# First SwiGLU block of a Hymba-style layer: the third of seven matmul products is issued ahead of the second

## The chip, the core and the metric

The kernel runs on one core of a Trainium2 chip. The time is device microseconds (us) of one launch, the median of several runs; shorter is better. The engines are named as in the profile: PE is TensorE (matmuls; PEld is its weight load, which overlaps), ACT is ScalarE, DVE is VectorE, POOL is GpSimd, and SP is the engine whose queue issues most transfers.

## What is computed

One decoder layer on 512 tokens of width 1024, in float32. Cut to what matters here:

```python
def swiglu(x, w_gate, w_up, w_down):
    return (jax.nn.silu(x @ w_gate) * (x @ w_up)) @ w_down

x = x + 0.5 * swiglu(rms_norm(x, g_ffn1), w_ffn1_gate, w_ffn1_up, w_ffn1_down)   # first SwiGLU block
h = rms_norm(x, g_mix); p = h @ w_in                                            # mixing stage:
x = x + concat(attention(p), conv(p), memory_attention(p, mem)) @ w_out         #   three head groups
x = x + 0.5 * swiglu(rms_norm(x, g_ffn2), w_ffn2_gate, w_ffn2_up, w_ffn2_down)   # second SwiGLU block
```

The hidden width D_FF is 2816, which is 22 blocks of 128.

## The kernel before

**Layout.** Activations are kept transposed: features lie on the 128 partitions and the 512 tokens along the free dimension. `x` has 8 such slices. Every float32 factor is split into a high part in the reduced format fp32r and the remainder (`whi`/`wlo` for weights, `bh`/`bl` for activations, `hh`/`hl` for hidden values), and each product is three matmuls: high times high, high times low, low times high.

**One SwiGLU block.** `ffn` loops over the 22 hidden blocks `f`. The first four (`N_DIRECT`) compute gate and up directly. The other 18 go through `fast`, which gets the gate and up values of one hidden block from seven products instead of eight, each over half the features and half the tokens (a Strassen-like scheme). A product is 4 steps of k with 3 matmuls each (lines 444, 445, 446): 12 matmuls of 128x256. In the text of `fast` the seven are, by the name of their activation block: `B_11`, `B_21`, `B_Q1`, `B_Q2`, `B_22`, `B_T4`, `B_T3`. They are called here by these names, without the B_.

**Which accumulator each one uses.** An accumulator bank is 128 partitions by 512 float32. `b` is half of one bank: product 11 fills it, `ACT.copy` (L455) reads it, Q2 is added to it, `ACT.copy` (L461) reads it again, T3 is added and DVE reads it (L475). `de` is a whole bank: product 21 fills its left half, Q1 its right half; `ACT.activation` (L459) reads the right half and writes its negative to `s45`; then 22 is added to the right half, and DVE reads all of `de` (L464). `c` is half of another bank (profile name `sc`) and takes T4. The profile calls `b` and `de` both `mm`, and `s12` and `s45` both `kept`.

**Which weights each one uses.** `W.next()` hands out one split weight tile: `w0` (raw gate weights) serves 11 and 21, `w1` (a sum of weights) serves Q1 and Q2, `w2` serves 22 and T3, `w3` serves T4. A call of `W.next()` also sees to it that the tile three places further on is loaded and split: a cast on ACT (L167), a subtraction on DVE (L168), sums of weights on DVE (L126 to L129), and a transfer issued on SP (L142). There are four slots of `whi`/`wlo` used in turn and four raw tiles. `w3` has a slot of its own (`vhi`/`vlo`).

**Between the products.** `mid` holds the down projections that are spread over the blocks from f = 8 on, and one at f = 5. Down projections of a block are 12 or 24 matmuls in lines 347 to 349: one after product 22, the others after T3. Some values of f also run hooks: preparations of the memory tokens (f = 12 to 18) and of the rotary table (from f = 19).

**Order.** The kernel is written as one program; a scheduler turns it into one queue per engine and puts in the waits between the engines. An instruction that is ready may be placed ahead of one that stands before it in the text. In the mixing stage the text's own order is the list `ORDER`, which begins:

```python
c c c c pM0 pM1 sumM c c facM pK c scoresM00 scoresM01 c softM01 softM00 weightsM0 c sumK c pV scoresM11
```

There `pM0` is a projection of 24 matmuls (L347 to L349), followed by a square on ACT (L817), `sumM` is 16 small matmuls (L826) that read these squares, and `pK` is the next projection.

Of the kernel before, what the change touches and what calls it, by code (L numbers as in the profile page):

```python
# [34 lines left out]
AF = mybir.ActivationFunctionType  # L35
# [47 lines left out]
B_T3, B_Q1, B_Q2, B_T4, B_21, B_22, B_11 = range(7)  # L83
# [124 lines left out]
def layer(tc, ctx, a):  # L208
    nc = tc.nc
    PE, ACT, DVE, POOL = nc.tensor, nc.scalar, nc.vector, nc.gpsimd  # L210
# [12 lines left out]
    def mm_bank():  # L223
        return psum.tile([P, T], F32, tag="mm", name=nm("mm"), bufs=4)

    def sc_bank():
        return psum.tile([P, T], F32, tag="sc", name=nm("sc"), bufs=2)
# [4 lines left out]
    def work():  # L232
        return tmp.tile([P, T], F32, tag="t", name=nm("t"), bufs=5)
# [160 lines left out]
    def ffn(pool, norm, first, gain, hooks, next_gain, last):  # L394
# [5 lines left out]
        def hidden(f, t):  # L400
            h_hi[f], h_lo[f] = atile("hh"), atile("hl")
            ACT.copy(h_hi[f], t)
            DVE.tensor_tensor(h_lo[f], t, h_hi[f].bitcast(F32), op=ALU.subtract)

        def kept():
            return pool.tile([P, T], F32, tag="kept", name=nm("kept"), bufs=3)
# [32 lines left out]
        def product(ps, w, woff, block, first):  # L439
            wh, wl = w  # L440
            for k in range(4):
                c = slice(woff + k * P, woff + (k + 1) * P)
                one, end = first and k == 0, k == 3
                PE.matmul(ps, wh[:, c], bh[k][:, block], start=one, stop=False, skip_group_check=not first)  # L444
                PE.matmul(ps, wh[:, c], bl[k][:, block], start=False, stop=False, skip_group_check=not first)  # L445
                PE.matmul(ps, wl[:, c], bh[k][:, block], start=False, stop=end, skip_group_check=not first)  # L446

        def fast(f, mid):

            l, r = slice(0, 256), slice(256, 512)  # L450
            b, de, c = mm_bank()[:, l], mm_bank(), sc_bank()[:, l]
            s12, s45, g, u = kept(), kept(), work(), work()
            w0 = W.next()
            product(b, w0, 0, B_11, True)
            ACT.copy(s12[:, l], b)  # L455
            product(de[:, l], w0, 512, B_21, True)
            w1 = W.next()
            product(de[:, r], w1, 0, B_Q1, True)
            ACT.activation(s45[:, r], de[:, r], AF.Copy, scale=-1.0)  # L459
            product(b, w1, 512, B_Q2, False)  # L460
            ACT.copy(s12[:, r], b)  # L461
            w2 = W.next()
            product(de[:, r], w2, 0, B_22, False)
            DVE.tensor_tensor(g, de, s12, op=ALU.add)  # L464
            ACT.activation(g, g, AF.Silu)
            rest = []
            for d in mid:
                rest += down(*d)
            if rest:
                rest.pop(0)()  # L470
            w3 = W.next()
            product(c, w3, 0, B_T4, True)
            ACT.copy(s45[:, l], c)
            product(b, w2, 512, B_T3, False)
            DVE.tensor_tensor(  # L475
                u.rearrange("p (a b) -> p a b", a=2), s45.rearrange("p (a b) -> p a b", a=2),
                b.unsqueeze(1).to_broadcast([P, 2, 256]), op=ALU.subtract,
            )
            DVE.tensor_tensor(u, u, g, op=ALU.mult)
            hidden(f, u)  # L480
            for d in rest:
                d()

        def down(r, g):

            lo, hi = ROUNDS[r]
            end = r == len(ROUNDS) - 1
            wh, wl = W.next()

            def step(j):  # L490
                d = g * per_load(r) + j
                cut = last and end and d == KT - 1
                for t0, t1 in [(0, T // 2), (T // 2, T)] if cut else [(0, T)]:
                    ps = mm_bank()[:, : t1 - t0]
                    mm3(
                        ps, wh, wl, range(lo, hi), lambda k: h_hi[k][:, t0:t1], lambda k: h_lo[k][:, t0:t1],
                        True, True, woff=lo - j * (hi - lo), cut=1 + (r > 0 and not cut),
                    )
                    xd = x[:, d, t0:t1]
                    if r == 0 and g < 2:  # L500
                        o = work()
                        ACT.activation(o, ps, AF.Copy, scale=0.5)
                        POOL.dma_start(xd, o, accum_op=ALU.add)
                        continue
                    o = work()[:, : t1 - t0] if last and end else xd
                    DVE.scalar_tensor_tensor(o, ps, 0.5, xd, op0=ALU.mult, op1=ALU.add)  # L506
                    if last and end:
                        nc.sync.dma_start(a["out"][d, :, t0:t1], o)
                if end and not last:
                    nxt.add(d)  # L510
                    scaled_split(d, next_gain)

            return [lambda j=j: step(j) for j in range(per_load(r))]
# [4 lines left out]
        for f in range(NF):  # L518
# [4 lines left out]
            if f >= N_DIRECT:  # L523
                fast(f, mid)
            else:
                g, u = (sc_bank(), sc_bank()) if f % 3 == 2 else (mm_bank(), mm_bank())
                gh, gl = W.next()
                if f == 0:
                    uh, ul = W.next()
                    for ks in first:  # L530
                        mm3(g, gh, gl, ks, xhk, xlk, ks[0] == 0, ks[-1] == 7)
                        mm3(u, uh, ul, ks, xhk, xlk, ks[0] == 0, ks[-1] == 7)
                    norm.stats()
                    held = (g, u)
                else:
                    mm3(g, gh, gl, range(8), xhk, xlk, True, True)
                    if f == 1:
                        norm.spread()
                        raw[0] = evac(0, *held)
                        blocks(0)  # L540
                        hidden(0, raw[0])
                    uh, ul = W.next()
                    mm3(u, uh, ul, range(8), xhk, xlk, True, True)
                    raw[f] = evac(f, g, u)
                    if f == 1:
                        hidden(1, raw[1])
                    blocks(f)
                if f == N_DIRECT - 1:
                    for i in range(2, N_DIRECT):
                        hidden(i, raw[i])  # L550
# [5 lines left out]
        r = len(ROUNDS) - 1  # L556
# [676 lines left out]
```

## Time and profile before

| | |
|---|---|
| runs (three) | 866.07, 872.06, 865.25 us; median 866.07 |
| profiled execution, own time | 870.17 us |
| its span (first to last instruction) | 868.1 us |
| mean granted TensorE clock | 1.000 |
| PE busy | 861.3 us (99%) |
| PEld busy | 795.1 us (92%) |
| DVE busy | 698.3 us (80%) |
| ACT busy | 446.0 us (51%) |
| read from HBM | 85.45 MB |
| fast part of the first SwiGLU block | about 70 to 344 us of the span |
| mixing stage | about 369 to 545 us |
| second SwiGLU block | about 545 us to the end |

How to read it: "busy" is the time in which an engine has an instruction in flight. Matmuls are pipelined, so a matmul of 0.28 us starts every 0.11 us or so, and TensorE's pace is read from the distance between starts, not from durations. A row of the timeline gives start (us), duration (us), engine, line, operation, output and inputs, shape and count; in square brackets stands the idle time of that engine ahead of the instruction, and what released it. A wait row gives the engine and line that waited, for whom, the total, the number of times and the longest.

### The profile page before, as it was taken

To read this page: it belongs to the slowest core of one execution; us is meant where nothing else is said; L and a number is where in the kernel's file an instruction comes from. 1 tells how busy PE (TensorE), PEld (TensorE's weight loads), DVE (VectorE), ACT (ScalarE), POOL (GpSimd) and SP (SyncE) were. 2 spreads that over 40 slices of the span, in tenths; PEclk is the share of its full clock that TensorE was granted. 3 is DMA by queue.
4 is the path that set the end of the run, shared out by engine and by line. 5 is a ranking of instruction groups with operands and counts; after the bars stand their busy time and mean duration, and the time that the engine had idled before them with its cause. 6 is when DMAs were issued, how large, how long until landed. Compare 5 with 4: busy or idle time off the path is not lost.

```text
span 868.1 us, 15720 instructions
## 1 busy us (share of the span) xinstructions
PE 861.3 (99%) x6361; PEld 795.1 (92%) x6361; DVE 698.3 (80%) x1163; ACT 446.0 (51%) x740; POOL 27.9 (3%) x30
## 2 busy tenths in 40 slices
PE   9999999999999999999999999999999999999998
PEld 5889999999999999988776878889999999999998
DVE  7998877777868887869989976997987878787772
ACT  7455545455554454632939754454554444545440
POOL 0010000000000000300000021010000000000000
PEclk9999999999999999999999999999999999999999
DMA  7326334334454344232020333336333333333312
GB/s 271 122 83 165 94 97 122 99 110 134 111 145 146 97 113 130 95 97 62 0 62 13 110 89 84 99 90 159 105 106 121 95 121 85 116 98 99 121 49 99
DMA packets 34809, 91.45 MB, mean 105 GB/s; under 512 B 3248, under 2 KB 5808, under 8 KB 34736
## 3 DMA queue, kind: packets, MB, share of 16 engines
q1 hardware_dynamic: 32000, 85.99, 32.1%
q0 software_dynamic: 1584, 2.88, 2.1%
q10 hardware_dynamic: 1152, 1.57, 0.7%
q8 instruction: 50, 0.82, 0.4%
q14 instruction: 23, 0.19, 0.1%
HBM read 85.45 MB, written 2.10 MB: 101 GB/s over the span
## 4 chain that ended last, share of the span: by engine, by line
PE 92%; DVE 3%; ACT 2%; issue 1%; DMA 1%; SPq 0%; ACTq 0%; DVEq 0%
PE mm L347 15%; PE mm L348 14%; PE mm L349 14%; PE mm L444 11%; PE mm L446 11%; PE mm L445 11%; PE sc L444 2%; PE sc L446 2%; PE sc L445 2%; PE sc L347 1%; PE sc L349 1%; PE sc L348 1%; PE tp L948 1%; PE tp L962 1%; ACT p L913 1%
## 5 line engine op out<-in xcount | busy, mean ns | idle before, releaser
L444 PE MATMUL mm<-bh,whi 128*128 128x256 f32 x864 | 239.9, 278 | 0.2 <-ACT kept L459 0.2
L446 PE MATMUL mm<-bh,wlo 128*128 128x256 f32 x864 | 239.6, 277 | 0.0
L445 PE MATMUL mm<-bl,whi 128*128 128x256 f32 x864 | 239.6, 277 | 0.0
L348 PE MATMUL mm<-hl,whi 128*128 128x256 f32 (+1 forms) x640 | 184.7, 289 | 0.0
L349 PE MATMUL mm<-hh,wlo 128*128 128x256 f32 (+1 forms) x640 | 184.6, 289 | 0.0
L347 PE MATMUL mm<-hh,whi 128*128 128x256 f32 (+1 forms) x640 | 184.1, 289 | 0.0
L167 ACT CAST whi<-wraw 128x1024 fp32r<-128x1024 f32 (+2 forms) x122 | 124.1, 1021 | 106.2 <-PE mm L348 45.0
L168 DVE TENSOR_TENSOR wlo<-wraw,whi 128x1024 fp32r<-128x1024 f32 (+2 forms) x122 | 145.4, 1193 | 34.4 <-ACT whi L167 34.0
L446 PEld LDWEIGHTS mm<-bh,wlo 128*128 128x128 f32 x864 | 163.1, 189 | 0.0
L444 PEld LDWEIGHTS mm<-bh,whi 128*128 128x128 f32 x864 | 162.2, 188 | 0.5 <-ACT kept L459 0.4
L445 PEld LDWEIGHTS mm<-bl,whi 128*128 128x128 f32 x864 | 162.2, 188 | 0.2
L349 PEld LDWEIGHTS mm<-hh,wlo 128*128 128x128 f32 x640 | 120.8, 189 | 2.9
L347 PEld LDWEIGHTS mm<-hh,whi 128*128 128x128 f32 x640 | 120.1, 188 | 2.7
L348 PEld LDWEIGHTS mm<-hl,whi 128*128 128x128 f32 x640 | 120.1, 188 | 2.7
L168 DVE TENSOR_TENSOR wlo<-s,whi 128x1024 fp32r<-128x1024 f32 x72 | 87.9, 1222 | 36.0 <-ACT whi L167 35.6
L167 ACT CAST whi<-s 128x1024 fp32r<-128x1024 f32 x72 | 75.5, 1050 | 47.3 <-PE mm L445 43.5
L348 PE MATMUL mm<-xl,whi 128*128 128x512 f32 x192 | 75.9, 395 | 0.6 <-DVE xl L359 0.5
L347 PE MATMUL mm<-xh,whi 128*128 128x512 f32 x192 | 76.3, 402 | 0.0
L349 PE MATMUL mm<-xh,wlo 128*128 128x512 f32 x192 | 75.8, 395 | 0.0
L506 DVE SCALAR_TENSOR_TENSOR x<-mm,x 128x512 f32<-128x512 f32 x80 | 54.0, 682 | 3.7 <-PE mm L349 3.7
L167 ACT CAST vhi<-wraw 128x512 fp32r<-128x512 f32 x36 | 22.4, 622 | 62.7 <-PE sc L445 48.5
L126 DVE TENSOR_TENSOR s<-wraw 128x512 f32<-128x512 f32 x36 | 24.9, 691 | 32.6 <-DMA wraw<-in_wgu 32.6
(243 smaller groups left out, 1368.3 us busy)
## 6 DMA issues: line engine op xcount, KB each, us to landing
wraw<-in_wgu SPq DMA_DIRECT2D x86, 512.0 KB, 3.6
wraw<-in_wd SPq DMA_DIRECT2D x44, 512.0 KB, 3.7
wraw<-in_win SPq DMA_DIRECT2D x12, 512.0 KB, 3.5
x<-t POOLq DMA_DIRECT2D x8, 256.0 KB, 6.1
out<-t SPq DMA_DIRECT2D x7, 256.0 KB, 2.0
x<-in_xT SPq DMA_DIRECT2D x3, 512.0 KB, 6.6
wraw<-in_wout_a SPq DMA_DIRECT2D x6, 256.0 KB, 2.7
wraw<-in_wgu SPq DMA_DIRECT2D x4, 256.0 KB, 4.9
```

Of the source, the lines that this page charges most:

```text
L126: nc.vector.tensor_tensor(s12[:, l], u[:, l], u[:, r], op=ALU.add)
L167: nc.scalar.copy(hi[:, :cols], raw[:, :cols])
L168: nc.vector.tensor_tensor(lo[:, :cols], raw[:, :cols], hi[:, :cols].bitcast(F32), op=ALU.subtract)
L347: PE.matmul(ps[:, t], wh[:, w], hi(k)[:, t], start=one, stop=False, skip_group_check=cut > 1)
L348: PE.matmul(ps[:, t], wh[:, w], lo(k)[:, t], start=False, stop=False, skip_group_check=cut > 1)
L349: PE.matmul(ps[:, t], wl[:, w], hi(k)[:, t], start=False, stop=end, skip_group_check=cut > 1)
L444: PE.matmul(ps, wh[:, c], bh[k][:, block], start=one, stop=False, skip_group_check=not first)
L445: PE.matmul(ps, wh[:, c], bl[k][:, block], start=False, stop=False, skip_group_check=not first)
L446: PE.matmul(ps, wl[:, c], bh[k][:, block], start=False, stop=end, skip_group_check=not first)
L506: DVE.scalar_tensor_tensor(o, ps, 0.5, xd, op0=ALU.mult, op1=ALU.add)
L913: ACT.activation(self.p[n, h][:, c], src[h][:, i, c], AF.Exp, scale=self.fac[:, m : m + 1], bias=self.neg[:, m : m + 1], accum_out=self.de ...
L948: PE.transpose(ps[:, i * P : (i + 1) * P], self.p[n, h][:, c : c + P], ident)
```

## The change

In `fast`, the call `w1 = W.next()` moves ahead of product 21 (in both SwiGLU blocks). In the first SwiGLU block (`last` is False), Q1 and the reading of its result (L459) then stand in the text ahead of product 21. All else keeps its order. Since Q1 now opens the bank `de`, product 21 is issued without the start flag there; its values are the same.

```diff
             product(b, w0, 0, B_11, True)
             ACT.copy(s12[:, l], b)
-            product(de[:, l], w0, 512, B_21, True)
             w1 = W.next()
-            product(de[:, r], w1, 0, B_Q1, True)
-            ACT.activation(s45[:, r], de[:, r], AF.Copy, scale=-1.0)
+            if last:
+                product(de[:, l], w0, 512, B_21, True)
+                product(de[:, r], w1, 0, B_Q1, True)
+                ACT.activation(s45[:, r], de[:, r], AF.Copy, scale=-1.0)
+            else:
+                product(de[:, r], w1, 0, B_Q1, True)
+                ACT.activation(s45[:, r], de[:, r], AF.Copy, scale=-1.0)
+                product(de[:, l], w0, 512, B_21, False)
             product(b, w1, 512, B_Q2, False)
             ACT.copy(s12[:, r], b)
             w2 = W.next()
```

## Prediction on record

> **What bounds the kernel now.** First the page's busy line and its chain of work, to see which engine sets the end.
>
> ```profile
> PE 861.3 (99%) x6361; PEld 795.1 (92%) x6361; DVE 698.3 (80%) x1163; ACT 446.0 (51%) x740; POOL 27.9 (3%) x30
> PE 92%; DVE 3%; ACT 2%; issue 1%; DMA 1%; SPq 0%; ACTq 0%; DVEq 0%
> ```
>
> TensorE is busy 99% of the span and is 92% of the chain. An edit that changes no matmul can therefore only win or lose TensorE's idle time, or change its pace. So the second view is the busy time of each engine in stretches; this row is the fast part of the first block.
>
> ```profile
> 70.00:344.00 274.00, 273.83 (x2336) 272.47 (x2335) 216.81 (x313) 138.91 (x214) 2.76 (x5) 1.00 0.41 119
> ```
>
> The columns after the length are PE, PEld, DVE, ACT, POOL with counts, then the granted clock. TensorE is busy 273.83 of 274.00 us: 0.17 us of visible idle time in all 18 blocks. The waits of TensorE and of its weight loads in 70:345 name the one place:
>
> ```profile
> PE mm L444 <- ACT kept L459: 0.2, 1, 0.2
> PEld mm L444 <- ACT kept L459: 0.4, 1, 0.4
> ```
>
> One wait, once: product 22 of block f = 8 waits for L459, the negated copy that frees the right half of `de`. The timeline there:
>
> ```profile
> 116.57 0.38 ACT L455 COPY kept<-mm 128x256 f32<-128x256 f32 x1
> 117.83 0.63 ACT L402 CAST hh<-t 128x512 fp32r<-128x512 f32 x1 [0.89 <-DVE t L479]
> 118.36 1.05 ACT L167 CAST whi<-wraw 128x1024 fp32r<-128x1024 f32 x1
> 119.31 0.37 ACT L459 ACTIVATE kept<-mm 128x256 f32<-128x256 f32 x1
> ...
> 119.29 0.28 PE L446 MATMUL mm<-bh,wlo 128*128 128x256 f32 x1
> 119.73 0.39 PE L444 MATMUL mm<-bh,whi 128*128 128x256 f32 x1 [0.17 <-ACT kept L459]
> 119.96 0.28 PE L445 MATMUL mm<-bl,whi 128*128 128x256 f32 x1
> ...
> 119.73 0.19 PEld L444 LDWEIGHTS mm<-bh,whi 128*128 128x128 f32 x1 [0.36 <-ACT kept L459]
> ```
>
> ACT was held up by L402, which waited for DVE; then came a cast; L459 ended at 119.68 and the weight load behind it began 0.05 later. At the usual step of 0.113 us (next fence) the row at 119.96 would have stood at 119.29 + 0.23 = 119.52: the wait costs 0.44 us.
>
> The third reading is TensorE's pace, from the counts in four stretches that hold no wait (the first also holds a few longer matmuls and isn't used):
>
> ```profile
> 70.00:119.00 49.00, 49.00 (x407) 47.83 (x406) 41.67 (x56) 27.64 (x44) 0.00 (x0) 1.00 0.39 114
> 120.00:270.00 150.00, 150.00 (x1276) 150.00 (x1276) 111.55 (x149) 74.70 (x119) 2.58 (x3) 1.00 0.40 118
> 283.00:343.00 60.00, 60.00 (x532) 60.00 (x531) 49.37 (x81) 27.85 (x43) 0.18 (x2) 1.00 0.39 114
> 630.00:760.00 130.00, 130.00 (x1150) 130.00 (x1149) 101.42 (x133) 65.48 (x100) 0.00 (x0) 1.00 0.36 107
> ```
>
> 150/1276 is 117.6 ns a matmul, 60/532 is 112.8 and 130/1150 is 113.0, with the clock at 1.00 and TensorE never idle in all three. The long step begins right behind the wait at 119.7. Over 1276 matmuls, 4.6 ns each are 5.8 us, thirteen times the wait itself. What makes a step long isn't shown; that it began with this wait may be chance, but it is the only wait and the only onset. So 6.2 us of the profiled 870.17 hang on one late L459.
>
> **The change part by part.** *Work.* Nothing is added or removed: 18 blocks of 84 matmuls stay, as do L455, L459 and L461. Sum: 0.
>
> *`w1 = W.next()` moves ahead of product 21, in both blocks.* With it move a cast on ACT, a subtraction on DVE, at times the sums of weights and a transfer on SP. What it passes, product 21, is TensorE's alone, so ACT's, DVE's and SP's queues keep this order: 0. In the second SwiGLU block that is all there is: 0, with no cover to lose.
>
> *Q1 runs a product earlier and 21 a product later, first block.* A product is 12 x 0.113 = 1.36 us. Q1 needs `w1` 1.36 us sooner, and the slot of `w0` comes free up to 1.36 us later, for the next tile. The tightest case is where that tile is the next block's own `w1`:
>
> ```profile
> 107.30 1.05 ACT L167 CAST whi<-s 128x1024 fp32r<-128x1024 f32 x1 [0.16 <-PE mm L445]
> ...
> 108.39 1.23 DVE L168 TENSOR_TENSOR wlo<-s,whi 128x1024 fp32r<-128x1024 f32 x1 [0.16 <-ACT whi L167]
> ```
>
> The cast follows the last reading of `w0` in f = 7 and the tile is split at 109.62. Working back from 119.29 at 1.36 us a product, Q1 of f = 8 starts at 116.68. With the change, split 110.98 and wanted 115.32: 4.3 us of slack are left, so 0. If that cover were gone, each microsecond late would be one of TensorE's. The transfer behind that slot shifts by as much, inside DVE's slack (216.81 busy of 274.00, 3.2 us free a block).
>
> *L455 against Q2.* Q2 may be added to `b` once L455 has read it. Two products lie between 11 and Q2 now. If Q2 follows Q1 directly there is one. In f = 8 L455 ends at 116.95 and Q2 would be wanted at 116.68: 0.3 us late. If 21 keeps its place ahead of Q2: 0.
>
> *L459 against 22.* Now one product of cover (Q2, 1.36 us); in the new text two (21 and Q2). L459 is ready 1.36 us sooner, and the cast ahead of it at 118.36 reads into the slot of `w0`, so it is ready only after 21 and drops behind L459. In f = 8 L459 could then end by 118.4 to 118.8, against 22 wanted at 119.40. The 0.44 us go, and with them, if the onset was no chance, the long step.
>
> *L459 against 21, a new wait.* 21 writes the left half of the bank whose right half L459 reads. The trace before has no row in which TensorE writes one half of a bank while ACT reads the other, so the cost is bounded. From below 0: no wait, or enough of Q2 put between. From above, nothing between, from f = 7:
>
> ```profile
> 108.41 0.28 PE L446 MATMUL mm<-bh,wlo 128*128 128x256 f32 x1
> 108.52 0.28 PE L444 MATMUL mm<-bh,whi 128*128 128x256 f32 x1
> ...
> 108.78 0.38 ACT L459 ACTIVATE kept<-mm 128x256 f32<-128x256 f32 x1 [0.43 <-PE mm L446]
> ```
>
> Q1's last matmul starts at 108.41, L459 ends at 109.16, and with 0.05 as at 119.73 the next matmul starts at 109.21 instead of 108.52: 0.69, and 0.11 for the restart (119.73 to 119.96 is 0.23, not 0.113) make 0.80 us a block, 14.4 us for 18. Behind 21 on TensorE stand 22, T4 and T3, and ACT and DVE wait for those. Seven matmuls of Q2 in between (0.8/0.113) hide it. Would they be put there? In the mixing stage the text has all 16 sums of `sumM` ahead of `pK`; the queue ran otherwise:
>
> ```profile
> 399.35 0.95 PE L826 MATMUL tp<-pair,t 128*128 128x2 f32 x8
> 400.16 0.48 PE L347 MATMUL mm<-xh,whi 128*128 128x512 f32 x1
> ...
> 401.40 0.39 PE L349 MATMUL mm<-xh,wlo 128*128 128x512 f32 x1
> 401.63 0.95 PE L826 MATMUL tp<-pair,t 128*128 128x2 f32 x8
> ...
> 400.32 0.59 ACT L817 ACTIVATE t<-mm 128x512 f32<-128x512 f32 x1
> ```
>
> Six matmuls of `pK` were put in while L817 was outstanding, and the second eight sums came 0.7 us after L817's end at 400.91: enough, with some over. I take 0, the nearest row, and keep 14.4.
>
> On this the Trainium skill, PSUM — Partial Sum Buffer, section "PSUM bank collisions raise a hardware error", speaks against the change: TensorE and ScalarE on one bank collide even at different columns, and the guard has to go by bank. By that rule the wait at 21 exists in each of the 18 blocks; no run here shows it yet.
>
> **Sum.** Against the profiled execution's 870.17: -0.44 - 5.8 = 863.9. The three runs are 865.25, 866.07 and 872.06. The third is 6.4 above the mean of the two others, 865.7, about the 6.2 of the late L459, so I estimate that the two ran without the long step and the profiled execution with it. Against a median of that kind there is little left to win. Forecast: between 863.9 and 865.7, **865.0**.
>
> **The rivals.** *A. Late in f = 8 all the same, and a long step behind it* (about 872). If L459 stays behind L402 on ACT, it takes the cast's place at 118.36 and ends at 118.73; 21 could start at 118.78. With Q1 over at 116.68, TensorE has 1.36 us of Q2 from 117.00 on and waits 0.4 us more, or 1.3 us in all with seven matmuls. So 0.9 to 1.4 us are lost instead of 0.44, and in every run: 865.7 + 5.8 + 1.1 = 872.6, or 870.9 from the profiled 870.17; 872. For it: the row at 117.83, L402 held by DVE. Against it: the cast ahead of L459 goes, and nothing says that L402 stays first.
>
> *B. Slower: TensorE waits for L459 at 21 in each block.* Place: the first weight load of 21; price 0.113 us for each matmul short of seven; it decides as soon as fewer are put in. None put in: 865.7 + 14.4 = 880.1, and with a long step through all 2336 matmuls (10.7 us) 890.8. Half the cover: 873. For it: the shared bank, the rule above. Against it: the sums at 401.63, with 0.7 us over.
>
> *C. The change doesn't do what it says:* TensorE's queue comes out in the old order, and nothing moves: 866.07. For it: as the sums show, a queue needn't follow the text. Against it: nothing keeps Q1 back, its weights are ready 4 us ahead.
>
> **How the numbers follow.** Forecast 0.45; A 0.25; B 0.18 (0.10 of it short waits, up to 876; 0.08 beyond); C 0.10; something faster than 863 0.02. The range is 863 to 876: from 0.9 below the sum against the profiled execution, through A, to the smaller half of B; outside lie B's upper part and the tail below, and part of each case's spread. A measurement of this kernel tells about 1% from no change, 8.7 us: 857.4 to 874.7 counts as the same. Forecast, C and nearly all of A lie inside, B from 5 matmuls short on lies above: faster 0.02, same 0.80, slower 0.18.
>
> **What would show it.** Right: in 70:344 no wait on L459 or L455, Q1's start 1.36 us into each block, and 113 ns a matmul throughout. A: one wait near f = 8 and 117.6 ns behind it. B: "PEld mm L444 <- ACT kept L459" 18 times, 0.1 to 0.7 us each. C: Q1 at 2.72 us into each block. Most likely to make me wrong: that the step's length depends on something other than this wait, or that L459 is placed badly on ACT.

## The result and the profile after

The changed kernel takes **874.78 us** (median of nine runs, 872.38 to 876.73) against 865.91 (nine runs, 865.25 to 872.06): the ratio is **1.0081**, 95% interval [1.0054, 1.0108]. The profiled execution took 875.49 us. First the page's busy line and its chain by engine:

```profile
PE 863.4 (99%) x6361; PEld 794.8 (91%) x6361; DVE 696.2 (80%) x1163; ACT 443.7 (51%) x740; POOL 27.9 (3%) x30
PE 92%; DVE 3%; ACT 2%; DMA 2%; issue 1%; SPq 0%; ACTq 0%; DVEq 0%
```

The counts are those of before: no work came or went. TensorE still sets the end, over a span of 873.2 instead of 868.1 us. To see where the 5.1 us lie, take a line that stands at the border of the first block and the mixing stage, the sums of squares of L378, in the view of one source line, of the kernel before and of the changed one:

```profile
L378 PE MATMUL tp<-ones,sqsum x8: 165/250/250, 376.0 to 376.7; 128*128 128x1 f32 x8
```

```profile
L378 PE MATMUL tp<-ones,sqsum x8: 165/250/250, 381.2 to 381.9; 128*128 128x1 f32 x8
```

They start 5.2 us later, so all of the difference had arisen by then, in the first block. The waits between 60 and 350 us name it (line numbers from the edit on are larger: L459 is now L463):

```profile
PEld mm L444 <- ACT kept L463: 4.9, 16, 1.1
PE mm L444 <- ACT kept L463: 0.9, 1, 0.9
PEld mm L444 <- ACT kept L455: 0.5, 1, 0.5
PE mm L444 <- ACT kept L455: 0.3, 1, 0.3
```

Where the weight load had one wait on the negated copy, it has 16. The timeline at f = 7 shows the usual one (start, duration, engine, line; the idle time before it in brackets):

```profile
108.14 0.28 PE L446 MATMUL mm<-bh,wlo 128*128 128x256 f32 x1
108.25 0.28 PE L444 MATMUL mm<-bh,whi 128*128 128x256 f32 x1
...
108.59 0.74 PE L444 MATMUL mm<-bh,whi 128*128 128x256 f32 x2
109.17 0.29 PE L445 MATMUL mm<-bl,whi 128*128 128x256 f32 x1
...
108.95 0.19 PEld L444 LDWEIGHTS mm<-bh,whi 128*128 128x128 f32 x1 [0.28 <-ACT kept L463]
...
108.51 0.39 ACT L463 ACTIVATE kept<-mm 128x256 f32<-128x256 f32 x1 [1.05 <-PE mm L446]
```

Q1's last matmul starts at 108.14, and ACT reads its result from 108.51 to 108.90. Between Q1 and 21 the queue holds **four** matmuls of Q2 (108.25 to 108.59), in this block and in 14 others; in the three blocks at 214, 230 and 245 us it holds five. The row with x2 is the last of them and 21's first, whose weights are loaded at 108.95, 0.05 us after the read. From 108.59 to 109.17 two steps take 0.58 us instead of 0.23: 0.35 lost. Two blocks lose more. The first fence is f = 8, the second f = 9:

```profile
118.48 0.28 PE L444 MATMUL mm<-bh,whi 128*128 128x256 f32 x1
119.68 0.39 PE L444 MATMUL mm<-bh,whi 128*128 128x256 f32 x1 [0.93 <-ACT kept L463]
...
117.03 0.37 ACT L455 COPY kept<-mm 128x256 f32<-128x256 f32 x1
118.73 0.62 ACT L402 CAST hh<-t 128x512 fp32r<-128x512 f32 x1 [1.32 <-DVE t L484]
119.25 0.38 ACT L463 ACTIVATE kept<-mm 128x256 f32<-128x256 f32 x1
```

```profile
134.19 0.28 PE L446 MATMUL mm<-bh,wlo 128*128 128x256 f32 x1
134.81 0.38 PE L444 MATMUL mm<-bh,whi 128*128 128x256 f32 x1 [0.34 <-ACT kept L455]
...
133.86 0.62 ACT L402 CAST hh<-t 128x512 fp32r<-128x512 f32 x1 [1.09 <-DVE t L484]
134.39 0.36 ACT L455 COPY kept<-mm 128x256 f32<-128x256 f32 x1
```

In both, L402 of the block before stands first on ACT and waits for DVE; in f = 8 it holds up L463 and 21, in f = 9 L455 and Q2. The stretches give the pace:

```profile
70.00:119.00 49.00, 48.44 (x390) 46.31 (x388) 39.35 (x54) 26.46 (x43) 0.00 (x0) 1.00 0.37 107
120.00:270.00 150.00, 149.33 (x1269) 147.72 (x1268) 108.44 (x145) 73.20 (x117) 2.58 (x3) 1.00 0.40 118
283.00:343.00 60.00, 59.74 (x519) 58.95 (x518) 49.20 (x80) 27.64 (x42) 0.00 (x0) 1.00 0.37 110
630.00:760.00 130.00, 130.00 (x1149) 130.00 (x1149) 103.06 (x136) 65.35 (x100) 0.00 (x0) 1.00 0.37 110
```

Before, the first three held 407, 1276 and 532 matmuls. To split waits from pace, I took the starts of all 128x256 matmuls between 70 and 346 us: what a gap has over its steps counts as wait (restart included), what is left over 113.3 ns a step as long step. The kernel before lost 1.9 us in waits and 5.9 in steps, the changed one 8.4 and 3.9. About 1.5 us of the waits are in every kernel below (memory preparation and transposes), so the new order costs about 6.4 us of waits, and its profiled execution had 2 us less of the long step than that of before. That difference gives 4.4 of the 5.1 us. The long step ran here from f = 9 (135 us) to 230 us at 117.8 ns a matmul, was 113.3 to 113.9 in the blocks behind that but for some 6 us at 274 us, which every kernel has (see the first experiment), and came back from 349 to 370 us (180 matmuls of 117.8 ns, 0.8 us over the short step): 5.2 in all, against 5.1 measured.

### The profile page after: what moved, and what is told of

Its sections match the earlier page's. It is cut to its first block, busy times and chain, and to the rows that moved or that the text cites. A ratio compares the mean times of both kernels' runs of the same rounds, so it can differ in the third digit from the quotient of the medians.

```text
span 873.2 us, 15709 instructions
## 1 busy us (share of the span) xinstructions
PE 863.4 (99%) x6361; PEld 794.8 (91%) x6361; DVE 696.2 (80%) x1163; ACT 443.7 (51%) x740; POOL 27.9 (3%) x30
## 4 chain that ended last, share of the span: by engine, by line
PE 92%; DVE 3%; ACT 2%; DMA 2%; issue 1%; SPq 0%; ACTq 0%; DVEq 0%
PE mm L347 15%; PE mm L349 15%; PE mm L348 15%; PE mm L444 11%; PE mm L445 10%; PE mm L446 10%; PE sc L445 2%; PE sc L446 2%; PE sc L444 2%; PE sc L347 1%; PE sc L349 1%; PE sc L348 1%; PE tp L953 1%; DMA wraw<-in_wgu 1%; PE tp L967 1%
## 5 line engine op out<-in xcount | busy, mean ns | idle before, releaser
L470 ACT ACTIVATE t<-t 128x512 f32<-128x512 f32 x36 | 22.8, 633 | 56.1 <-DVE t L469 56.1
```

## The experiments

The two theories set against each other from the start: the loss is the wait at 21 for the half-read bank (price: what is short of seven matmuls), or it lies elsewhere, in the moved call, in ACT's order, or in TensorE's pace itself. The times of before in these comparisons are medians of 865.6 to 866.04 us. The split into waits and long step is the one just explained.

### Only the call moved

```diff
-            product(de[:, l], w0, 512, B_21, True)
             w1 = W.next()
+            product(de[:, l], w0, 512, B_21, True)
```

> Only the call of W.next for w1 stands ahead of 21, in both blocks; the products keep the old order. The prediction priced this at 0: 865.9, within 1 us of the kernel before, with the same single wait near f = 8 at most. If the earlier call is what costs (an ACT or DVE queue in another order), it shows here: 868 or more.

Measured: 865.34 us (864.01 to 872.25), ratio 1.0000 [0.9978, 1.0022]. Waits 1.5, long step 0.3 in the profiled execution (864.01 us). The moved call costs nothing, in either block.

This trace also closes the account of the changed kernel, whose profiled execution took 11.5 us more. Its waits are 6.9 us more (8.4 against 1.5), its long step up to 346 us 3.6 more, and the long step from 349 to 370 us adds 0.8: 11.3.

The view of waits names none in this trace between 60 and 350 us. Yet one stretch is at the long step, behind eight small matmuls of the memory preparation:

```profile
263.50 0.95 PE L615 MATMUL tp<-ones,mtot 128*128 128x1 f32 x8
264.30 0.36 PE L347 MATMUL mm<-mh,whi 128*128 128x256 f32 x1
264.74 0.28 PE L347 MATMUL mm<-mh,whi 128*128 128x256 f32 x1
...
270.04 0.29 PE L646 MATMUL mm<-whi,mh 128*128 128x256 f32 x1
```

From 264.74 to 270.04 us there are 45 steps of 117.8 ns; with the products of L646 the step is 113.3 again. Every trace of this case has such a stretch. Whether the break or this kind of product makes it long isn't shown.

### Q2 whole ahead of 21

```diff
                 product(de[:, r], w1, 0, B_Q1, True)
                 ACT.activation(s45[:, r], de[:, r], AF.Copy, scale=-1.0)
+                product(b, w1, 512, B_Q2, False)
                 product(de[:, l], w0, 512, B_21, False)
-            product(b, w1, 512, B_Q2, False)
```

> Order in the first block: 11, Q1, all twelve matmuls of Q2, then 21. T1 (21 waits for L459 because both use one bank, and only four matmuls of Q2 stand between): twelve cover the 0.8 us, so the 0.37 us a block go, 6 to 7 us of the 8.9, leaving one late block or two (f = 8, 9): 866 to 868. T2 (ACT is late because L402 and casts stand ahead of L459, whatever the bank): 21 still waits, 872 to 875. T3 (the loss is the long matmul step, whatever the waits): the step stays at 117 to 118 ns in a long stretch, 870 to 875.

Measured: 870.0 us, ratio 1.0029 [1.0006, 1.0053]; the twelve runs lie between 864.75 and 871.85. With twelve matmuls between Q1 and 21, no wait on the negated copy is left between 70 and 346 us. What is left in the profiled execution (871.72 us) begins at f = 9:

```profile
132.16 0.34 PE L444 MATMUL mm<-bh,whi 128*128 128x256 f32 x1
132.34 0.28 PE L445 MATMUL mm<-bl,whi 128*128 128x256 f32 x1
...
131.17 0.62 ACT L402 CAST hh<-t 128x512 fp32r<-128x512 f32 x1 [0.55 <-DVE t L485]
131.69 0.37 ACT L455 COPY kept<-mm 128x256 f32<-128x256 f32 x1
...
132.11 0.19 PEld L444 LDWEIGHTS mm<-bh,whi 128*128 128x128 f32 x1
```

```profile
100.00:131.00 31.00, 31.00 (x276) 31.00 (x275) 25.41 (x33) 17.71 (x28) 0.00 (x0) 1.00 0.35 110
133.00:260.00 127.00, 127.00 (x1080) 127.00 (x1080) 94.95 (x126) 65.41 (x104) 2.58 (x3) 1.00 0.40 119
```

L402 held up L455, which ended at 132.06. Q2's first weights were loaded 0.05 us after that, and its second matmul started 0.07 us late (0.18 between two starts instead of 0.113). Ahead of it a matmul takes 31.00/276 = 112.3 ns, behind it 127.00/1080 = 117.6, with TensorE busy throughout. Waits 1.6, long step 5.5: a stall of 0.07 us stands at the head of 5.2 of the 7.7 us by which this execution is longer than that of the first experiment. So the waits went as T1 expects, but the time came out where T3 has it, by the long step.

### 21 in another bank

```diff
-                product(de[:, l], w0, 512, B_21, False)
+                product(bank[:, r], w0, 512, B_21, False)   # bank[:, l] is b
...
-            DVE.tensor_tensor(g, de, s12, op=ALU.add)
+                DVE.tensor_tensor(g[:, l], bank[:, r], s12[:, l], op=ALU.add)
+                DVE.tensor_tensor(g[:, r], de[:, r], s12[:, r], op=ALU.add)
```

> The changed order, but 21 goes into the free half of the bank of b, so it shares no bank with what L459 reads; L464 becomes two instructions of 256 columns. T1: no wait on L459 ahead of 21, and 22 has two products of cover; what can be left is 21 or Q2 waiting for L455 in f = 8 or 9, under 1 us: 864.5 to 867.5. T2: waits on ACT stay, 870 to 875. T3: the time follows the step, not the bank: anything up to 872.

Measured: 869.52 us (865.21 to 871.12), ratio 1.0018 [0.9994, 1.0042]. The waits between 60 and 350 us of TensorE and its weight loads:

```profile
PEld mm L444 <- ACT kept L456: 0.8, 1, 0.8
PE mm L444 <- ACT kept L456: 0.6, 1, 0.6
PEld mm L444 <- DVE t L473: 0.2, 1, 0.2
```

None is on the negated copy, though here 21 follows Q1 directly. L456 is the copy of product 11, which reads the other half of the bank that 21 now uses; it was held by L402 once, at 147 us, and the long step followed until 269 us (waits 2.7, long step 4.9). So it is the shared bank that makes 21 wait. The time, 2 us over T1's range, again holds the long step. The Trainium skill, PSUM — Partial Sum Buffer, section "PSUM bank collisions raise a hardware error", asks for a guard by bank even where the columns differ. These traces agree, in that the waits go by bank: with the bank shared there is one in each block whose cover is short, with another bank none on the copy of Q1. It is the scheduler that puts these waits in, and no run leaves one out.

### Six of Q2 ahead of 21, and none

```diff
-        def product(ps, w, woff, block, first):
+        def product(ps, w, woff, block, first, ks=range(4)):
...
+                product(b, w1, 512, B_Q2, False, range(2))      # 6 matmuls
                 product(de[:, l], w0, 512, B_21, False)
-            product(b, w1, 512, B_Q2, False)
+            product(b, w1, 512, B_Q2, False, range(4) if last else range(2, 4))
```

> The changed order with six matmuls of Q2 ahead of 21 by the text, where the changed kernel has four and e1 twelve. T1: each matmul is 0.113 us of cover, so the wait of 0.37 us a block falls to about 0.14, 4 us less in 18 blocks; f = 8 and 9 stay late: 869 to 872 and 16 or so short waits on L459. T2 (ACT late for other reasons): the waits stay at 0.37, 873 to 876. T3 (the step alone): times between 866 and 875 whatever the waits.

```diff
-                product(de[:, l], w0, 512, B_21, False)
-            product(b, w1, 512, B_Q2, False)
+                p21 = product(de[:, l], w0, 512, B_21, False)
...
+                with tc.issue_after(p21.ins):    # queued behind 21: Q2, the block's down projection, T4
+                    product(b, w1, 512, B_Q2, False)
```

> The changed order, but Q2, T4 and the block's down projection are queued on TensorE behind 21 in the first block, so that from f = 7 to f = 21 (15 blocks) nothing stands between Q1 and 21, and four matmuls in f = 4 to 6. Theory (21 waits until the bank's other half has been read; price 0.113 us for each matmul short of seven): 15 waits of 0.7 to 0.8 us on the copy of Q1 and 3 of 0.35, 12 to 13 us in all, against 18 of 0.35 in the changed kernel; with the long step in none to most of the stretches 864.5 + 12.5 + 0 to 9, that is 877 to 887 us. Rival (the wait is a fixed 0.35 us whatever stands between, or the loss lies in something else than this wait): 873 to 877 us.

Measured with six: 872.11 us, ratio 1.0068 [1.0042, 1.0095]; waits 4.1, long step 3.7. With none: 879.35 us (878.71 to 880.35), ratio 1.0139 [1.0098, 1.0179]; waits 14.2, long step 1.7. The timeline of a block in each, six first:

```profile
108.75 0.28 PE L446 MATMUL mm<-bh,wlo 128*128 128x256 f32 x1
108.92 0.38 PE L444 MATMUL mm<-bh,whi 128*128 128x256 f32 x1
109.14 0.28 PE L445 MATMUL mm<-bl,whi 128*128 128x256 f32 x1
```

```profile
135.64 0.28 PE L446 MATMUL mm<-bh,wlo 128*128 128x256 f32 x1
136.45 0.39 PE L444 MATMUL mm<-bh,whi 128*128 128x256 f32 x1 [0.53 <-ACT kept L464]
136.67 0.28 PE L445 MATMUL mm<-bl,whi 128*128 128x256 f32 x1
...
136.01 0.38 ACT L464 ACTIVATE kept<-mm 128x256 f32<-128x256 f32 x1 [0.92 <-PE mm L446]
```

Two steps take 0.39 us with six between and 1.03 with none, instead of 0.23: 0.16 and 0.80 lost, and 0.35 with four in the changed kernel. In the other blocks with six it is 0.05 to 0.13, but for 0.85 in the late f = 8, which is the only one that the view of waits names. The price falls by about 0.11 us a matmul put in, as in the prediction. The waits with none between:

```profile
PEld mm L444 <- ACT kept L464: 10.7, 16, 0.7
PE mm L444 <- ACT kept L464: 7.3, 14, 0.5
```

Fourteen of the 16 are of the full length. In f = 4 and f = 6 four matmuls of another product still came between (0.35 each). In f = 7 a matmul put in between waited itself, for late weights (0.6 us), and in f = 17 eight small matmuls of the memory preparation covered the read. So the expectation's count was not quite met, and the waits came to 12.7 us over the common 1.5.

### L402 and L403 later on ACT: in the kernel before, the changed kernel, and with Q2 first

In all three, the split of a block's hidden values (L402 and L403) is queued behind the negated copy of the next block:

```diff
+            neg = ACT.activation(s45[:, r], de[:, r], AF.Copy, scale=-1.0)
+            while pend:
+                with tc.issue_after(neg.ins):
+                    hidden(*pend.pop(0))
...
-            hidden(f, u)
+            if last:
+                hidden(f, u)
+            else:
+                pend.append((f, u))
...
```

> The kernel before, but in the first block the split of the hidden values (L402) is queued on ACT behind L459 of the next block, so that neither L455 nor L459 can be held up by DVE in f = 8 or later. If late ACT work is what makes TensorE wait there and the wait starts the long step: no wait, 113 ns throughout, 863.5 to 865.5 in every run. If the long step comes by itself: some runs stay at 870 to 872 and the median is that of before.

> The changed kernel with the same shift of L402 behind L459. T1: the 0.37 us a block at 21 stay, 6.5 us, and only the late blocks f = 8 and 9 (1.2 and 0.6 us) go: 870 to 871 with the short step, up to 876 where the step is long. T2 (ACT late is the whole loss): 864 to 866.

> In the first block Q1, then the whole of Q2, then 21 (as when Q2 was put whole ahead of 21), and besides L402 and L403 of a block are queued on ACT behind the L464 of the next block. Theory (the new order costs only by TensorE's wait at 21 for a shared bank; what was left over with Q2 first, 0.07 us at f = 9 and a long step behind it, came from L402 holding up L455 on ACT): no wait of TensorE of over 0.05 us on a `kept` copy between 70 and 346 us, 113 ns a matmul in 130:260 (about 1150), 864.5 us, all runs within 864 to 867. Rival (the order itself makes the step long, or costs in some other way, with no wait to be seen): still a long step in 130:260 (1104 to 1110 matmuls) or times of 869 to 872 in most runs.

Measured: in the kernel before **864.68 us**, twelve runs between 864.39 and 866.62 where that kernel itself, in the same call, ranged from 864.57 to 871.5; ratio 0.9983 [0.9966, 1.0001], waits 1.9, long step 0.3. Its timeline at f = 8 and its stretch:

```profile
118.45 0.39 ACT L459 ACTIVATE kept<-mm 128x256 f32<-128x256 f32 x1 [0.42 <-PE mm L446]
118.73 0.62 ACT L402 CAST hh<-t 128x512 fp32r<-128x512 f32 x1
```

```profile
130.00:260.00 130.00, 130.00 (x1150) 130.00 (x1149) 102.12 (x133) 68.20 (x109) 2.59 (x3) 1.00 0.44 128
```

L459 waits only for Q1, the wait of f = 8 is gone, and the step is 113.0 ns. One wait of 0.3 us is left, of a down projection at 338 us, and the step behind it stays short. The same edit does not help the changed kernel: 875.41 us, ratio 1.0107 [1.0086, 1.0127], waits 7.6, long step 4.2. There all 18 blocks now have nearly the same wait (0.28 to 0.36 us with the restart):

```profile
PEld mm L444 <- ACT kept L463: 4.8, 18, 0.3
```

So the late L402 in f = 8 and f = 9 wasn't what made the changed kernel slow. The long step came behind 8 of these 18 waits and not behind the others, so the length of a wait does not decide it. With Q2 whole ahead of 21 the edit gives 865.2 us, ratio 0.9985 [0.9963, 1.0007]; waits 1.9, long step 0.3, no wait on L455 or L464. Eleven of twelve runs lie between 864.16 and 866.02, one at 872.95; of that one there is no trace. The order that the change wanted therefore costs nothing that these runs can tell once 21 is covered and ACT isn't held up. It gains nothing either: the kernel before with L402 later is the best version, by little, and the interval just includes no change.

### A failed mend: the first down projection ahead of 22, in the kernel before

```diff
+            if rest and not last:
+                rest.pop(0)()
             product(de[:, r], w2, 0, B_22, False)
...
-            if rest:
+            if rest and last:
```

> The kernel before, with the first down projection of each block of the first SwiGLU block put ahead of product 22 instead of behind it, so that L459 has 2.8 us more cover from f = 8 on. If the late L459 of f = 8 is what starts the long step in the kernel before, there is no wait and the step stays at 113 ns from 70 to 344: 864 to 865.5 in every run, none at 870 to 872. If the long step comes by itself, it appears here too in some runs, and the time is 865 to 872 as before.

Measured: 873.92 us, ratio 1.0093 [1.0069, 1.0117]; waits 7.8, long step 3.1. The cover for 22 moved the trouble to Q2, so neither reading of the expectation is tested by it:

```profile
PEld mm L444 <- ACT kept L455: 5.0, 7, 1.9
```

### One wait, alone, in the second SwiGLU block

The kernel before, with the changed product order in one block of the 36, f = 10 of the second SwiGLU block. The call `w1 = W.next()` stands ahead of 21 in all blocks, as in the first experiment:

```diff
-            product(de[:, l], w0, 512, B_21, True)
             w1 = W.next()
+            if not last or f != 10:
...                                        # as before: 21, Q1
+            else:
...                                        # as changed: Q1, 21
```

> The kernel before with the new product order in one block only, f = 10 of the second SwiGLU block, where no wait stands before and the step is 113 ns to the end. The order alone costs one wait of about 0.4 us: 866.3. If a wait can start the long step, the step behind it is 117 to 118 ns in some runs, and those are up to 8 us longer (some 1700 matmuls at 4.5 ns): 866 and 870 to 874 mixed. If the long step has another cause: all within 1 us of before.

Measured: 874.76 us (six runs, 872.13 to 878.06), ratio 1.0102 [1.0078, 1.0126]. The one wait in the profiled execution (872.13 us), and the stretches ahead of and behind it:

```profile
660.45 0.74 PE L444 MATMUL mm<-bh,whi 128*128 128x256 f32 x2
661.03 0.28 PE L445 MATMUL mm<-bl,whi 128*128 128x256 f32 x1
...
660.80 0.19 PEld L444 LDWEIGHTS mm<-bh,whi 128*128 128x128 f32 x1 [0.28 <-ACT kept L463]
```

```profile
610.00:660.00 50.00, 50.00 (x444) 50.00 (x443) 41.73 (x55) 27.08 (x43) 0.00 (x0) 1.00 0.36 106
662.00:860.00 198.00, 198.00 (x1684) 198.00 (x1683) 141.03 (x180) 86.91 (x129) 0.00 (x0) 1.00 0.32 96
```

The wait is 0.35 us. Ahead of it a matmul takes 50.00/444 = 112.6 ns, behind it 198.00/1684 = 117.6, to the end, at a granted clock of 1.00 and with TensorE never idle. Its first SwiGLU block was at the short step but for the stretch at 264 us, and its span, 870.0, is 8.1 us over the 861.9 of the kernel in which only the call moved: one wait of 0.35 us and 1684 steps of 4.6 ns. None of the six runs was under 872 us, so the mix of 866 and 870 to 874 that was expected did not come. Two runs, at 876.03 and 878.06, lost more than the wait and one long step to the end give; they have no trace. The traced run is the plainest evidence that a wait of TensorE can start the long step and that it is no property of the first block.

## Why the prediction was wrong, point by point

**The step that failed is the cost of L459 against 21.** It was put between 0 and 14.4 us and taken as 0, by the sums' row at 399 to 402 us, where six matmuls had been put in with 0.7 us to spare. That row shows that something is put in while a copy is outstanding; it does not show that enough is. Here four of the needed seven matmuls came in 15 blocks and five in three. The waits of the 18 blocks come to 6.9 us (0.16 to 0.35 in sixteen of them, 1.19 in f = 8 and 0.6 in f = 9) against 0.44 before: that is the growth of the waits by about 6.4.

**The price was right.** 0.80 us with nothing between, less 0.113 for each matmul, gives 0.80, 0.35, 0.24, 0.12 and 0 for none, four, five, six and twelve. Measured were 0.80, 0.35, 0.16 to 0.24, 0.05 to 0.16 and 0. So the mechanism was rival B, near half of the cover. That its times came so close is in part luck. "Half the cover 873" has 7.2 us of waits and no long step; the changed kernel, at 874.78, has slightly smaller waits and 4 to 5 us of long step in its trace. "None put in 880.1" has 18 full waits; the 879.35 has 14 and some others. Why four or five are put in wasn't tried.

**The long step** was sized rightly: the profiled execution of the first experiment, which had no wait at f = 8, took 864.01 us, 6.2 less than that of before. That a wait can start it is borne out by the single wait at 660 us, though a wait need not, and the stretch at 264 us is long behind no wait that the view names. What failed with the step above is that it would go: each new wait can start it or end it. In the changed kernel it took 3.9 us of the profiled execution up to 346 us.

**L459 against 22.** The wait at 22 went, as forecast. But that L459 drops in ahead of the cast did not free it: L402 stayed first in f = 8, as rival A had it. A put the loss there at 0.9 to 1.4 us; from 118.48 to 119.90 two steps take 1.42 us instead of 0.23, 1.19 lost. Its long step behind that wait did not come; the step stayed at 113.5 ns until f = 9.

**L455 against Q2.** The forecast's 0.3 us in f = 8 did not show: Q2 started at 118.14 and the copy was over at 117.40. Four earlier waits of 0.35 us had put Q2 back by 1.4 us, so this is no test of the estimate. The same lateness came in f = 9, as 0.51 us (134.19 to 134.81, less a step), because L402 was held there.

**The moved call, and Q1's weights**: 0, as forecast; moving the call alone changed nothing, and in the changed kernel no wait of TensorE between 60 and 350 us is on a weight tile.

**The median.** That two of the first three runs were at the short step and the profiled one at the long fits what followed: with the wait at f = 8 removed, the times came to 864.68 with no run above 866.62. Of the kernel before, only the profiled execution has a trace. The change of 0.81% is within the 1% to which most of the chance went, but its interval, 0.54 to 1.08%, excludes no change, and it lies on the slow side, where the forecast had 865.0. The 874.78 us lie inside the stated 863 to 876 by the allowance for A and for short waits of B, not by the mechanism of the forecast.

**Still open:** what makes the step long or short after a wait. Waits as short as 0.05 us (348.4 us of the changed kernel) were followed by it, one of over 1 us (f = 8 of the same kernel) was not, and of 18 nearly equal ones 8 were.

## What to carry to other kernels

Where a product fills the other half of a bank that ACT still reads, count the matmuls that the queue really holds between the two, and compare with the time from the last matmul to the end of the read (0.8 us here, seven matmuls). Putting the whole of another product between them, or using another bank, removes the wait; relying on the queue to fill in is a forecast to be read off the queue, not off another stage. And where TensorE is 99% busy, a single short wait is not priced by its own length: look at the starts behind it.

## What the runs showed of the hardware that was not expected

In these traces a stream of 128x256 matmuls in this format runs at one of two paces, 113.3 or 117.8 ns a matmul, both at a granted clock of 1.00 and with TensorE shown as busy. The long pace, once begun, lasted at least to the next break in the stream (1684 matmuls in one case), but for 270 us, where another kind of product ended it. It began behind waits, some as short as 0.05 us, but not behind each, and at 264 us of the first experiment behind eight small matmuls, without a wait that the view names. In this kernel that turns stalls of a few tenths of a us into 4 to 8 us. It would also explain why the times of the kernel before fall mostly near 865 and near 871 us: its traced execution, at 870.17, has the one stall and the long pace behind it; its executions near 865 have no trace.
